# Attention in steps of four heads: the value product in plain float32, one key group in each half of TensorE's columns

## The chip, the cores and the metric

The kernel runs on one core of a Trainium2 chip. The metric is the device time of one execution in microseconds (us); lower is better. The engines are TensorE (PE for its matmuls, PEld for its weight loads), VectorE (DVE), ScalarE (ACT) and GpSimd (POOL); SyncE (SP) issues the DMAs.

## What is computed

Two layers of a backbone over 1024 latent and 256 context tokens of width 1024. The part that matters here is the attention of a layer: eight query heads of width 64 in two key groups, four heads to a group.

```python
def gqa_softmax(qg, k, v):
    s = jnp.einsum('bqgrd,bkgd->bgrqk', qg, k, preferred_element_type=jnp.float32) * (HEAD_DIM ** -0.5)
    p = jax.nn.softmax(s, axis=-1).astype(v.dtype)
    return jnp.einsum('bgrqk,bkgd->bqgrd', p, v)

def reference(...):
    for i in range(DEPTH):
        ...
        # latent queries read context and latent keys (1280), in both layers
        latent_attention(q, k, v, kc, vc)
        ...
        if update_ctx:      # layer 0 only: context queries read the 256 context keys
            context_attention(qc, kc, vc)
        ...
```

All arrays are float32. Pooling and Fourier mixers, an output projection, and a SwiGLU FFN fill the rest of a layer.

## The kernel before

**One list of operations, one planner.** The whole kernel is written as operations with an engine (or a choice of engines), a cost, and a rank; `Plan.run` (class at L53) takes them in order of time and rank and gives each engine its fixed sequence. `SHIFTS` holds an offset of rank for each name and layer, `ENGINES` the engines that a name may use, `ORDER` and `QUERY` the offsets inside one attention step. Buffers are slots that an operation takes and a later one gives back: pages of SBUF, two banks `t0`/`t1` for transposed tiles, one bank `sc` for context scores, one bank `pv` for the value product, two double banks `x0`/`x1` for latent scores.

**Most products are made in three parts.** TensorE multiplies float32 numbers that are split into a rounded high part (type F32R, "fp32r") and a rest (`mm3`, L473 to L475: low by high, high by low, high by high).

**Attention (from L1419).** A step is one *pair*: 128 queries (`t`), one key group `g`, two heads (`h0`, `h0`+1). A layer has 8 blocks of 128 latent queries, so 32 latent pairs; layer 0 has 8 context pairs more. For each pair:

- SC and SA/SB (`Pair.product`, L1502): scores, 4 matmuls of 256 columns for the context keys into `ps_sc`, and per head 4 of 512 columns into `ps_s`.
- MC, ML (L1511, L1431), N (L1435): maxima on DVE, and from them the bias of the exponential.
- EC, EL (L1441, L1447): exponentials on ACT, into `pc`/`pd` (context) and `p` (latent), with the row sums. R (L1517, L1518): reciprocal of the sum.
- T (L1461): five blocks of four 128x128 transposes, so that the keys lie in the partitions; each block of four is one bank `ps_t`.
- For blocks 0, 2 and 4 (`DIRECT`): ACT casts the bank to a high part `ph` (C), and DVE subtracts it from the bank for the low part (G). For blocks 1 and 3: ACT copies the bank to `pt` (C), ACT, DVE or POOL casts it (H), and POOL subtracts (G).
- V (L1484): the stationary operand is 128 columns wide, 64 columns of the values' high part and 64 of their low part for one group; the moving operand is 256 columns (two heads), once the high part, once the low part. So 20 matmuls for a latent pair, which run through all 128 columns of the array.
- F (L1523): the reciprocals are spread over 64 partitions by a float32 matmul with the identity, one per head, the two heads in the two column halves of the array.
- O (L1527), A (L1530), X (L1535): ACT copies the low half of `ps_pv`, DVE adds the high half and multiplies by the spread reciprocals.

The values are split into high and low parts once per layer (`value_chain`, L1001). The conditioning vector's products (`ada`, L560, matmul at L579) are float32 matmuls with a stationary operand of 32 columns, four of them side by side in the four quarters of the array; they are named because the prediction reads a price from them.

Of the kernel before, what the change touches and what calls it, by code (L numbers as in the profile page):

```python
# [17 lines left out]
P = 128  # L18
# [213 lines left out]
def ns_tt(n):  # L232
    return 68 + 1.043 * n
# [14 lines left out]

def ns_copy_psum(n):
    return 65 + 1.043 * n  # L250
# [16 lines left out]
def setting(table, name, default):  # L267
# [10 lines left out]

DIRECT = (0,2,4)
SPLIT = ()  # L280
OUT = "A"

DEFAULT = {"copy": "AD", "turn": "A", "sum": "DG", "shift": "AG", "square": "A"}
ENGINES = {"C": "A", "G": "G", "H": "ADG", "O": "A", "act hi": "A", "act lo": "DG", "act sum": "D", "eh": "AD", "el": "G",
# [5 lines left out]
           "pool lo": "D", "rope add": "DG", "rope cos": "DG", "rope sin": "DG", "square": "A", "sum": "D",  # L290
           "u hi": "G", "u lo": "DG", "v copy": "D", "v hi": "A", "w hi": "A", "w lo": "DG", "w sum": "DG",
           "x hi": "A", "x lo": "DG", "x shift": "AD", "x sum": "D"}

SHIFTS = ({"A": -523400, "C": -318500, "EC": -222000, "EL": -91800, "F": -234400, "G": -1299600, "H": -339200, "MC": -541600,
           "ML": -175000, "N": -423300, "O": -18300, "R": -17500, "SA": -9300, "SB": -491400, "SC": -1584400,
           "T": -718800, "V": 7200, "X": -457600, "aa": -1187200, "act hi": -456000, "act lo": -1226900,
           "act sum": 125700, "ada": -147400, "ada add": -15300, "ada row": -33000, "ada sum": 20100,
           "ada total": -857400, "ada turn": 12900, "as": 342600, "channels": -614600, "dft": -598800,
# [69 lines left out]
def tile_backbone(ctx: ExitStack, tc: tile.TileContext, i, out, x_spill, act_spill):  # L368
# [443 lines left out]
    def layer(l, x, hx, last_load):  # L812
# [188 lines left out]
        def value_chain(pair, o, first, e):  # L1001
# [11 lines left out]
            for j, ch in enumerate(pair):  # L1013
# [11 lines left out]
                def high(e, tag, b=b, v=v):  # L1025
                    v.t = page(tag, [n // P, 2, P], F32R, "v")
                    copy(e, v.t[:, :, :, 0:64], both(b.t))
# [1445 lines left out]
```

## Time and profile before

| | |
|---|---|
| time, median of 3 runs | 2696.35 us (2694.25 to 2696.66) |
| the profiled execution | 2692.95 us |
| its span, from the first instruction to the last | 2691.2 us |
| PE busy / DVE busy / ACT busy / POOL busy | 2589.1 / 2197.5 / 1302.1 / 723.0 us |
| mean granted TensorE clock | 0.987 of full speed |

How to read it: a row of a timeline gives start, duration, engine, source line, operation, output and input tiles and the number of merged instructions. The ends of matmuls are modelled and overlap, so the pace of TensorE is read from the distance between starts. A float32 matmul that isn't a transpose leaves two records; an fp32r matmul and a transpose leave one.

### The profile page before, as it was taken

Reading aid. Unit: us, or ns where it says so; the run is one execution under the profiler, and the core shown is the slowest. Engines: PE = TensorE matmul, PEld = TensorE weight load, DVE = VectorE, ACT = ScalarE, POOL = GpSimd, SP = SyncE. Lnnn points to the kernel's source line nnn. Section 1 sums busy time; section 2 is a strip of 40 time slices with the busy share of each in tenths; the row PEclk is TensorE's granted clock in tenths of the full one; section 3 lists DMA queues with packets and bytes.
Section 4 is the critical chain, followed back from the end, with each engine's and each line's share of the span. In section 5 each row is a group of like instructions: output and inputs, shape, how many; then the busy total and the mean of one; then the engine's idle time right before and its main releaser. Section 6 shows DMA issues by size and latency. Waiting matters only on the chain.

```text
span 2691.2 us, 39675 instructions
## 1 busy us (share of the span) xinstructions
PE 2589.1 (96%) x14670; PEld 2188.3 (81%) x14670; DVE 2197.5 (82%) x3681; ACT 1302.1 (48%) x2418; POOL 723.0 (27%) x578
## 2 busy tenths in 40 slices
PE   6999998998999999999999999999998999999999
PEld 5888887777788888888888888888876788888887
DVE  6765888889969988776788987888899977777886
ACT  4225987746522222233444534799846333333442
POOL 2113543464301100000223323444434401010240
PEclk8999999999999999999999999999998999999999
DMA  7244100245244445427534323000152332325733
GB/s 281 87 136 131 36 1 1 74 133 175 83 168 139 159 154 170 145 81 261 173 98 123 105 92 110 21 1 1 58 179 97 133 131 89 118 83 193 242 98 121
DMA packets 126210, 314.90 MB, mean 117 GB/s; under 512 B 14784, under 2 KB 23360, under 8 KB 126016
## 3 DMA queue, kind: packets, MB, share of 16 engines
q1 hardware_dynamic: 126016, 312.36, 34.9%
q8 instruction: 116, 1.90, 0.3%
q14 instruction: 78, 0.64, 0.1%
HBM read 244.94 MB, written 62.13 MB: 114 GB/s over the span
## 4 chain that ended last, share of the span: by engine, by line
PE 69%; DVE 18%; ACT 7%; issue 3%; DMA 3%; POOL 0%; SPq 0%; DVEq 0%; ACTq 0%; POOLq 0%
PE ps_s L473 7%; PE ps_s L474 7%; PE ps_s L475 7%; PE ps_d L474 5%; PE ps_d L473 5%; PE ps_d L475 5%; DVE half L463 3%; PE ps_pv L1484 3%; PE ps_in L473 3%; PE ps_in L474 3%; PE ps_in L475 3%; PE ps_t L1461 3%; PE ps_s L1502 2%; ACT p L1447 2%; DVE ws L463 2%
## 5 line engine op out<-in xcount | busy, mean ns | idle before, releaser
L460 ACT CAST half<-ws 128x512 fp32r<-128x512 f32 x410 | 246.5, 620 | 505.9 <-PE ps_s L475 220.5
L473 PE MATMUL ps_s<-half 128*128 128x512 f32 x1056 | 417.5, 395 | 15.4 <-DVE half L463 8.9
L474 PE MATMUL ps_s<-half 128*128 128x512 f32 x1056 | 416.3, 394 | 1.9 <-POOL half L463 1.2
L475 PE MATMUL ps_s<-half 128*128 128x512 f32 x1056 | 414.5, 393 | 0.0
L463 POOL TENSOR_TENSOR ws<-wst 128x512 f32<-128x512 f32 x95 | 147.2, 1551 | 922.2 <-DVE half L463 791.0
L473 PE MATMUL ps_d<-half 128*128 128x512 f32 (+1 forms) x792 | 290.0, 366 | 1.2 <-ACT half L460 1.2
L474 PE MATMUL ps_d<-half 128*128 128x512 f32 (+1 forms) x792 | 289.7, 366 | 1.0 <-DVE half L463 1.0
L475 PE MATMUL ps_d<-half 128*128 128x512 f32 (+1 forms) x792 | 289.5, 365 | 0.0
L463 DVE TENSOR_TENSOR half<-ws,half 128x512 fp32r<-128x512 f32 x324 | 232.9, 729 | 52.0 <-ACT half L460 49.6
L473 PEld LDWEIGHTS ps_s<-half 128*128 128x128 f32 x1056 | 200.7, 190 | 61.7 <-DVE half L463 9.9
L474 PEld LDWEIGHTS ps_s<-half 128*128 128x128 f32 x1056 | 200.5, 190 | 47.0 <-DVE half L463 3.4
L475 PEld LDWEIGHTS ps_s<-half 128*128 128x128 f32 x1056 | 200.6, 190 | 41.7
L463 POOL TENSOR_TENSOR ph<-pt,ph 128x512 fp32r<-128x512 f32 x128 | 164.2, 1283 | 234.2 <-DVE ph L460 105.7
L460 ACT CAST half<-wst 128x512 fp32r<-128x512 f32 x224 | 132.5, 618 | 191.5 <-PE ps_s L475 88.6
L1484 PE MATMUL ps_pv<-ph,v 128*128 128x256 f32 x1312 | 199.5, 291 | 4.3 <-DVE mix L1535 3.6
L463 POOL TENSOR_TENSOR half<-ws,half 128x512 fp32r<-128x512 f32 x86 | 122.2, 1429 | 263.5 <-ACT half L460 220.3
L1484 PEld LDWEIGHTS ps_pv<-ph,v 128*128 128x128 f32 x1312 | 174.2, 190 | 13.3 <-issue 3.2
L463 DVE TENSOR_TENSOR ws<-wst 128x512 f32<-128x512 f32 x235 | 166.4, 723 | 10.4 <-DMA wst<-in_w_gate_up 4.9
L473 PEld LDWEIGHTS ps_d<-half 128*128 128x128 f32 x792 | 149.4, 189 | 25.9 <-ACT half L460 1.6
L474 PEld LDWEIGHTS ps_d<-half 128*128 128x128 f32 x792 | 149.4, 189 | 25.4 <-DVE half L463 1.4
L475 PEld LDWEIGHTS ps_d<-half 128*128 128x128 f32 x792 | 149.4, 189 | 24.0
L463 DVE TENSOR_TENSOR half<-wst,half 128x512 fp32r<-128x512 f32 x211 | 142.0, 697 | 30.7 <-ACT half L460 30.6
(271 smaller groups left out, 6296.7 us busy)
## 6 DMA issues: line engine op xcount, KB each, us to landing
wst<-in_w_gate_up SPq DMA_DIRECT2D x99, 512.0 KB, 4.5
ast<-in_w_ada SPq DMA_DIRECT2D x96, 512.0 KB, 3.9
as<-act_spill SPq DMA_DIRECT2D x165, 256.0 KB, 2.7
hs<-in_w_out SPq DMA_DIRECT2D x96, 256.0 KB, 3.1
act_spill<-c SPq DMA_DIRECT2D x44, 512.0 KB, 5.1
wst<-in_w_down SPq DMA_DIRECT2D x44, 512.0 KB, 6.2
x_spill<-x SPq DMA_DIRECT2D x28, 512.0 KB, 3.1
x<-x_spill SPq DMA_DIRECT2D x26, 512.0 KB, 6.3
```

What stands on the lines that cost most here:

```text
L460: (nc.scalar.copy if e == "A" else nc.vector.tensor_copy)(out, x)
L463: (nc.vector if e == "D" else nc.gpsimd).tensor_tensor(out, x, y, op)
L473: nc.tensor.matmul(o, wl, xh, start=start, stop=False)
L474: nc.tensor.matmul(o, wh, xl, start=False, stop=False)
L475: nc.tensor.matmul(o, wh, xh, start=False, stop=stop)
L1447: nc.scalar.activation(self.p, self.s, AF.Exp, bias=pr.col(2, h), scale=rq[pr.at][:, h:h + 1], accum_out=pr.col(4, h))
L1461: nc.tensor.transpose(self.t[:, 2 * q + h, :], src, ident)
L1484: nc.tensor.matmul(pr.pv, v, m[:, 2 * q:2 * q + 2, :].rearrange("p h c -> p (h c)"), start=(self.k0 + q == 0 and j == 0), stop=(self.k0 + ...
L1502: nc.tensor.matmul(o, self.q[0][:, self.h0 + h, :], kv["k", k0](self.g, j), start=(j == 1), stop=(j == 0))
```

## The change

- A step is now a *quad*: two heads of both groups (`Quad`), made of two pairs. A layer has 16 latent quads; layer 0 has 4 context quads more.
- Values stay float32 and unsplit (`v out` in place of `v hi` and `v lo`), in two pages for a layer in place of three.
- Each transposed block is only copied, to a page `pt` that both groups share (C, on ACT or DVE). H, G and A are gone, with their buffers.
- V multiplies float32 by float32: for each tile of 128 keys one matmul for group 0 into partitions 0 to 63 of the bank and one for group 1 into partitions 64 to 127, each with 64 stationary and 256 moving columns. It is issued in two batches, blocks 0 and 1, then blocks 2, 3 and 4 with the spread F behind them (`BATCHES`).
- O copies 128 partitions at once, X multiplies once for the quad.
- Rings of buffers: `p` 5 (was 4), `ph` 7 (was 5), `qs` 4 in two pages (was 2), statistics `mx` 4 of double width; the page `b6` joins the rooms for `p` and `ph`.
- Nearly all numbers of `SHIFTS` and 32 entries of `ENGINES` are new, for the whole kernel; `ORDER` and `QUERY` are the same. One line of it:

```diff
-ENGINES = {"C": "A", "G": "G", "H": "ADG", "O": "A", "act hi": "A", "act lo": "DG", "act sum": "D", "eh": "AD", "el": "G",
+ENGINES = {"C": "AD", "G": "G", "H": "ADG", "O": "AD", "act hi": "A", "act lo": "D", "act sum": "D", "eh": "D", "el": "DG",
```

The core of the rest:

```diff
+def ns_fp32(n):
+    return 0.833 * n + 2
+NS_MODE = 300
-DIRECT = (0,2,4)
+BATCHES = ((0, 1), (2, 3, 4))
...
-                hi = op("turn", n, high, [t, pool_done[1]], take=[{256: "b5", 768: "b6", 0: "b7"}[ch]], name="v hi")
-                lo = op("D", ns_tt(n), lambda b=b, v=v: nc.vector.tensor_sub(
-                    v.t[:, :, :, 64:128], both(b.t), v.t[:, :, :, 0:64].bitcast(F32)), [hi], give=[t], name="v lo")
...
+                out_ = op("turn", n, lambda e, b=b, dst=dst: copy(e, dst(), b.t), [t, v.op], give=[t], name="v out")
...
-            def high(self, e, tag, x):
...
-            def low(self, e, x):
-                combine(e, self.l, x, self.h.bitcast(F32), ALU.subtract)
-            def values(self, *tag):
...
-                for q in range(2):
-                    v = kv["v", ch].t[:, self.k0 + q - ch // P, pr.g, :]
-                    for j, m in enumerate((self.h, self.l)):
-                        nc.tensor.matmul(pr.pv, v, m[:, 2 * q:2 * q + 2, :].rearrange("p h c -> p (h c)"),
...
+        class Quad:
...
+            def values(self, k0s, end, *tag):
...
+                for k0 in k0s:
+                    ch = max(c for c in SIZE if c <= k0 * P)
+                    for q in range(2):
+                        v = kv["v", ch]()[:, k0 + q - ch // P, :]
+                        for g in range(2):
+                            own = slice(64 * g, 64 * g + 64)
+                            nc.tensor.matmul(self.bank[own, 0:2 * P], v[:, own], self.pt[k0][:, g, 2 * P * q:2 * P * q + 2 * P],
+                                             start=(k0 + q == 0), stop=(k0 + q == self.nkt - 1))
...
+                if end:
+                    self.spread()
+            def spread(self):
+                for h in range(2):
+                    for g in range(2):
+                        r = self.small[:, 12 * g + 10 + h:12 * g + 11 + h]
+                        nc.tensor.matmul(self.bank[64 * g:64 * g + 64, (2 + h) * P:(3 + h) * P], r.to_broadcast([P, 64]), ident,
+                                         start=True, stop=True)
...
-        for ch, t, g in [(ch, t, g) for ch in ((256, 768) if last else CHS)
-                         for t in range(0, SIZE[ch], P) for g in range(2)]:
+        for ch, t in [(ch, t) for ch in ((256, 768) if last else CHS) for t in range(0, SIZE[ch], P)]:
...
+                        cp = mk("C", "turn", 512, bl.copy, tr, *turned.get(b, [])[:1], j=b, take=[ring("ph"), rooms] if g == 0 else (),
+                                give=[tr])
...
+                for bs in BATCHES if ch else ((0,),):
+                    end = bs[-1] == len(pr.blocks) - 1
+                    lv = mk("V", "PE", 4 * len(bs) * ns_fp32(2 * P) + NS_MODE + 4 * end * ns_fp32(P),
```

How the instructions move, in three places. In all of them `ps_t` is a transposed block, `ps_pv` the value product, `ps_s` and `ps_sc` latent and context scores.

TensorE, in the attention of layer 1. Before, most of one pair, from its second block of latent transposes on:

```order
L1461 MATMUL ps_t<-ident,p 128x128 x4
L1502 MATMUL ps_s<-kd,qs 128x512 x4
L1484 MATMUL ps_pv<-ph,v 128x256 x4
L1461 MATMUL ps_t<-ident,p 128x128 x8
L1484 MATMUL ps_pv<-ph,v 128x256 x8
L1523 MATMUL ps_pv<-ident,smalls 64x128 x2
```

Now, the second half of a quad:

```order
L1529 MATMUL ps_sc<-kd,qt 128x256 x4
L1529 MATMUL ps_s<-kd,qt 128x512 x2
L1466 MATMUL ps_t<-ident,pc 128x128 x4
L1466 MATMUL ps_t<-ident,p 128x128 x4
L1529 MATMUL ps_s<-kd,qt 128x512 x4
L1466 MATMUL ps_t<-ident,p 128x128 x8
L1490 MATMUL ps_pv<-pt,v 64x256 x12
L1500 MATMUL ps_pv<-ident,smalls 64x128 x4
```

The value product stood in three pieces between transposes and scores, 20 matmuls for a pair. Now 12 follow each other directly, with the four spreads behind them; the other 8 of the quad stand two blocks of transposes earlier. In the built order of layer 1 the matmuls of L1490 carry a wait of their own in 5 places; elsewhere the transposes ahead of them already waited for the copies that freed their banks.

ScalarE, in the attention of layer 1 (`p` and `pc`, `pd` are the exponentials). Before:

```order
L1447 ACTIVATE p,smalls<-ps_s,smalls,rq 128x1024
L460 CAST ph<-ps_t 128x512
L460 COPY pt<-ps_t 128x512
L460 CAST ph<-pt 128x512
L1441 ACTIVATE pd,smalls<-ps_sc,smalls,rq 128x256
```

Now:

```order
L466 COPY pt<-ps_t 128x512
L1446 ACTIVATE pc,smalls<-ps_sc,smalls,rq 128x256
L1452 ACTIVATE p,smalls<-ps_s,smalls,rq 128x1024
L466 COPY pt<-ps_t 128x512 x2
L1446 ACTIVATE pd,smalls<-ps_sc,smalls,rq 128x256
```

The two casts to `ph` are gone. Over the kernel ACT had 200 casts from `ps_t`, 128 copies of it and 48 casts of `pt`; now it has 212 copies, and DVE has 116.

GpSimd, towards the end of the attention of layer 0, where the queries of the context come. Before:

```order
L463 TENSOR_TENSOR qs<-mix,qs 64x256 x2
L463 TENSOR_TENSOR ph<-pt,ph 128x512 x3
L463 TENSOR_TENSOR qs<-mix,qs 64x512
L463 TENSOR_TENSOR ph<-pt,ph 128x512 x2
L458 TENSOR_SCALAR ph<-pt 128x512
```

Now, at the same place:

```order
L469 TENSOR_TENSOR half<-mix,half 128x512
L469 TENSOR_TENSOR qt<-mix,qt 64x256 x4
L469 TENSOR_TENSOR qs<-mix,qs 64x512 x2
L469 TENSOR_TENSOR qt<-mix,qt 64x512 x2
L469 TENSOR_TENSOR half<-mix,half 128x512 x3
```

The 128 subtractions for `ph` and 11 casts are gone from POOL; of attention it keeps the low parts of the queries (`qs`, `qt`).

## Rows read from the trace of the kernel before

**Rows 1.** The profile's page: busy time by engine (share of the span, instructions), TensorE's busy tenths and the granted clock in 40 slices of the span, and the shares of the chain of work that ended last.

```profile
PE 2589.1 (96%) x14670; PEld 2188.3 (81%) x14670; DVE 2197.5 (82%) x3681; ACT 1302.1 (48%) x2418; POOL 723.0 (27%) x578
...
PE   6999998998999999999999999999998999999999
...
PEclk8999999999999999999999999999998999999999
...
PE 69%; DVE 18%; ACT 7%; issue 3%; DMA 3%; POOL 0%; SPq 0%; DVEq 0%; ACTq 0%; POOLq 0%
```

**Rows 2.** Busy time in three stretches of attention, the first two in layer 0, the third in layer 1. Columns: stretch, length, busy us (and instructions) of PE, PEld, DVE, ACT, POOL, then granted clock, DMA share and GB/s.

```profile
300.00:400.00 100.00, 97.74 (x705) 83.89 (x704) 87.23 (x190) 90.07 (x188) 46.76 (x44) 1.00 0.01 1
400.00:500.00 100.00, 89.11 (x618) 76.14 (x618) 87.26 (x170) 78.77 (x165) 37.48 (x36) 0.98 0.02 6
1750.00:1850.00 100.00, 98.56 (x706) 84.18 (x705) 86.81 (x192) 92.26 (x193) 43.87 (x40) 1.00 0.00 1
```

**Rows 3.** The same three stretches for the value product alone (line L1484): PE, PEld, clock, DMA share, GB/s.

```profile
300.00:400.00 100.00, 38.99 (x260) 34.21 (x261) 1.00 0.01 1
400.00:500.00 100.00, 34.22 (x218) 29.13 (x218) 0.98 0.02 6
1750.00:1850.00 100.00, 38.01 (x254) 33.18 (x253) 1.00 0.00 1
```

**Rows 4.** Timeline of TensorE over one latent pair of layer 1: start, us, engine, line, operation, tiles, stationary and moving shape, count.

```profile
1806.40 0.44 PE L1523 MATMUL ps_pv<-ident,smalls 128*64 128x128 f32 x4
1806.77 0.66 PE L1461 MATMUL ps_t<-ident,p 128*128 128x128 f32 x4
1807.45 1.20 PE L1502 MATMUL ps_s<-kd,qs 128*128 128x512 f32 x4
1808.52 0.74 PE L1502 MATMUL ps_sc<-kd,qs 128*128 128x256 f32 x4
1809.11 0.27 PE L1461 MATMUL ps_t<-ident,pd 128*128 128x128 f32 x1
1809.21 0.27 PE L1461 MATMUL ps_t<-ident,pc 128*128 128x128 f32 x1
...
1809.46 1.20 PE L1484 MATMUL ps_pv<-ph,v 128*128 128x256 f32 x8
1810.50 0.60 PE L1461 MATMUL ps_t<-ident,p 128*128 128x128 f32 x4
1810.85 1.17 PE L1502 MATMUL ps_s<-kd,qs 128*128 128x512 f32 x4
1811.86 0.64 PE L1484 MATMUL ps_pv<-ph,v 128*128 128x256 f32 x4
1812.34 1.04 PE L1461 MATMUL ps_t<-ident,p 128*128 128x128 f32 x8
1813.13 1.20 PE L1484 MATMUL ps_pv<-ph,v 128*128 128x256 f32 x8
1814.26 0.44 PE L1523 MATMUL ps_pv<-ident,smalls 128*64 128x128 f32 x4
1814.63 0.66 PE L1461 MATMUL ps_t<-ident,p 128*128 128x128 f32 x4
```

**Rows 5.** Timeline of TensorE early in the run, around the float32 products of `ada` in four column quarters.

```profile
21.35 0.64 PE L579 MATMUL ps_ada<-ast,cond 128*32 128x128 f32 x16 [0.41 <-DVE rows L588]
...
22.24 1.52 PE L579 MATMUL ps_ada<-ast,cond 128*32 128x128 f32 x48
```

**Rows 6.** Timeline of TensorE where such products stand alone between fp32r matmuls of 512 columns.

```profile
200.51 0.39 PE L474 MATMUL ps_in<-parts,w 128*128 128x512 f32 x1
200.74 0.39 PE L475 MATMUL ps_in<-parts,w 128*128 128x512 f32 x1
201.06 0.64 PE L579 MATMUL ps_ada<-ast,cond 128*32 128x128 f32 x16
201.63 0.50 PE L473 MATMUL ps_in<-parts,w 128*128 128x512 f32 x1
```

**Rows 7.** Groups of instructions by line with the shapes kept apart: busy us, mean ns of one, idle time before them and what ended it.

```profile
L1431 DVE TENSOR_REDUCE smalls<-ps_s 128x1 f32<-128x1024 f32 x128 | 155.8, 1218 | 6.3 <-PE ps_s L1502 6.1
...
L460 ACT CAST ph<-ps_t 128x512 fp32r<-128x512 f32 x200 | 116.7, 585 | 20.1 <-PE ps_pv L1484 10.1 <-PE ps_t L1461 9.7
...
L463 POOL TENSOR_TENSOR ph<-pt,ph 128x512 fp32r<-128x512 f32 x128 | 164.2, 1283 | 234.2 <-DVE ph L460 105.7 <-ACT ph L460 102.1 <-issue 23.2
L1447 ACT ACTIVATE p<-ps_s,smalls,rq 128x1024 f32<-128x1024 f32 x128 | 155.9, 1218 | 0.1
...
L463 DVE TENSOR_TENSOR ph<-ps_t,ph 128x512 fp32r<-128x512 f32 x200 | 137.4, 687 | 24.2 <-ACT ph L460 18.1 <-POOL ph L463 0.5
...
L1441 ACT ACTIVATE pc<-ps_sc,smalls,rq 128x256 f32<-128x256 f32 x90 | 50.8, 565 | 16.8 <-DVE smalls L1435 11.4 <-PE ps_pv L1523 3.6 <-DVE smalls L1513 0.4
```

**Rows 8.** Timeline of all engines at one moment in layer 0's attention, GpSimd's and VectorE's rows.

```profile
406.13 1.28 POOL L463 TENSOR_TENSOR ph<-pt,ph 128x512 fp32r<-128x512 f32 x1 [4.87 <-ACT ph L460]
...
406.27 1.17 DVE L1435 SCALAR_TENSOR_TENSOR smalls<-smalls,nrq 128x1 f32<-128x1 f32 x1
```

**Rows 9.** Timeline of VectorE in layer 1's attention: the same operation as in the second row of the group above.

```profile
1812.35 0.21 DVE L1435 SCALAR_TENSOR_TENSOR smalls<-smalls,nrq 128x1 f32<-128x1 f32 x1
```

More of the change, by code (lines that the diff above doesn't have):

```diff
@@ L1575, in layer @@
             for h0 in (0, 2):
-                pr = Pair(ch, t, g, h0, q)
+                quad = Quad(ch, t, h0)
+                pairs = [Pair(quad, g, qs[g]) for g in range(2)]
                 def mk(kind, eng, ns, f, *after, j=0, take=(), give=(), alone=None):
@@ L1602, in layer @@
-                uses["k"][1].extend(read)
-                uses["k"][0].extend(read if ch else ())
-                join(ex, [(sc, 0)])
-                rc = mk("R", "D", 260, pr.recip, *ex, *el)
-                lv = None
-                first_v = None
-                for b, bl in enumerate(pr.blocks):
-                    tr = mk("T", "PE", 436, bl.transpose, *(el if b else ex), j=b, take=[TB])
-                    if b == 0:
-                        join([tr], ex)
-                    if b in DIRECT:
-                        hi = mk("C", "A", 478, lambda _, tag, bl=bl: bl.high("A", tag, bl.t), tr, j=b, take=[ring("ph"), rooms])
-                        lo = mk("G", "D", ns_tt(512), lambda bl=bl: bl.low("D", bl.t), hi, j=b, give=[tr], alone=True)
-                    else:
-                        cp = mk("C", "turn", 512, bl.copy, tr, fixed["pt"].op, j=b, take=[ring("pt")], give=[tr])
-                        hi = mk("H", "copy", 512, lambda e, _, tag, bl=bl: bl.high(e, tag, bl.pt), cp,
-                                j=b, take=[ring("ph"), rooms])
-                        lo = mk("G", "sum", 512, lambda e, bl=bl: bl.low(e, bl.pt), hi, j=b, give=[cp])
-                    lv = mk("V", "PE", 436, bl.values, lo, lv, *vd, j=b, take=["pv"] * (b == 0), give=[hi])
@@ new lines, in layer @@
+                lv = first_v = None
+                for bs in BATCHES if ch else ((0,),):
+                    end = bs[-1] == len(pr.blocks) - 1
+                    lv = mk("V", "PE", 4 * len(bs) * ns_fp32(2 * P) + NS_MODE + 4 * end * ns_fp32(P),
+                            lambda *tag, bs=bs, quad=quad, end=end: quad.values([2 * b for b in bs], end, *tag),
+                            *[c for b in bs for c in turned[b]], lv, *vd, *(rc if end else ()), j=bs[-1], take=["pv"] * (lv is None))
@@ L1621, in layer @@
                     first_v = first_v or lv
+                    join([lv], [turned[b][0] for b in bs])
                     uses["v"][1].append(lv)
                     uses["v"][0].extend([lv] if ch else ())
[L1624 to L1629 removed]
@@ L1630, in layer @@
-                join([fx_], [(sc, 1)])
+                o = mk("O", "turn", 256, quad.copy, lv, take=[ring("o")])
+                fx_ = mk("X", "D", ns_tt(256), quad.scale, o, give=[first_v, o])
+                join([fx_], [(small, 1)])
                 att.setdefault((ch, t), []).append(fx_)
-                n += 1 if ch else 0.4
-            join(read, [qh])
+            for g in range(2):
+                join(read[g], [qh[g]])
         plan.t = TB0 + 7000 * n
```

233 lines of the change are left out of this document (119 added, 114 removed), and 53 rows, old and new, of tables (ENGINES, SHIFTS).

## Prediction

> **What bounds the kernel now.** I read the page first. TensorE is busy for 96% of the span at nearly full clock, and of the chain that ended last 69% is TensorE's, 18% VectorE's [rows 1]. So only what shortens TensorE's sequence, or a wait in it, can pay, and I look for the stages where it is not packed. The change rewrites attention, so the stretches of attention come next. In layer 1, and in layer 0 from 300 to 400 us, three engines are nearly full at once: in 100 us TensorE is busy for 98, ScalarE for 90 to 92, VectorE for 87 [rows 2]. Such a stage turns in a ring: the scores wait for an exponential's buffer, the exponential queues behind casts on ScalarE, its bias behind subtractions on VectorE. From 400 to 500 us all is slower: TensorE 89, ScalarE 79 [rows 2], and 218 value matmuls pass instead of 260 [rows 3]. At 20 for a pair that is 10.9 pairs instead of 13.0, so 2.1 pairs of 100/13.0 = 7.7 us, or 16 us, are lost there.
>
> The timeline of one pair gives TensorE's prices [rows 4]. From 1806.77 to 1814.63 it takes 7.86 us. The value product takes 1.04 (1809.46 to 1810.50), 0.48 (1811.86 to 1812.34) and 1.13 (1813.13 to 1814.26), together 2.65; the spread takes 0.37 (to 1814.63). All the rest, scores and transposes, takes 7.86 - 3.02 = 4.84.
>
> **The change, part by part.** *A. Value product and spread on TensorE.* Two pairs become one quad: 2 x 3.02 = 6.04 us go. What comes is float32 products in two column halves, and the trace has the same kind in four quarters. There 16 records take 0.64 us and 48 take 1.52 [rows 5]: 32 records, 16 matmuls, four sets of four, in 0.88, so 0.22 for a set of 128 columns. That is what one fp32r matmul of 512 columns takes (200.51 to 200.74, 0.23) [rows 6]. The spread of today is two float32 matmuls in two halves, and 0.37 later TensorE is at the next transpose [rows 4]; one after the other they would need 2 x 0.22 before any change of shape is paid. So I take halves to overlap as quarters do: a set of two matmuls of 256 columns costs 0.44. The bounds are 0.44 and, with no overlap, 0.88; nothing lower, since 256 columns cannot pass sooner than twice 128. Going into such products and out of them costs too: alone between two others, two sets take from 200.74 to 201.63 = 0.89, of which 0.23 is the matmul before them and 0.44 the sets, so 0.22 for a visit [rows 6]. I take 0.22; the bounds are 0 and 0.5. A quad has 10 sets in two visits, and two sets of 0.22 for the spread in the second: 4.40 + 0.44 + 0.44 = 5.28. That saves 0.76, in 32 latent quads 24 us. A context quad goes from 2 x (4 x 0.1325 + 0.37) = 1.80 (a value matmul being 2.65/20) to 0.88 + 0.44 + 0.22 = 1.54; four of them save 1. **A: -25 us.**
>
> One rule of the skill speaks against this price. The rows show a set of four in the time of one, 0.22 [rows 5]. The Trainium skill, in "TensorE: Matmul & The Clock Gate", section "Measured speedup vs the span model", gives a speedup of 2.38 for three column tiles, which is 79% of three. As an estimate from that page a set would take 0.44/0.79 = 0.56, and the sum would come to about 2690 instead of 2651.
>
> *B. Waits in the ring.* By the built order ScalarE's 376 casts and copies of transposed blocks become 212; at 0.585 us [rows 7] the 164 gone are 96 us, 2.7 for each of the 36 quads. VectorE loses 200 subtractions of 0.687 and gains 116 copies, which I price like them (a read of the same bank): -58 us, and the additions and 69 casts besides. From about 90% of a quad both fall below 80%, so TensorE alone should set the pace. What can that give? The 4.84 us for the rest of a pair hold 20 transposes 0.11 apart (1809.11, 1809.21), 8 matmuls at 0.23 and 4 at half of that: 2.2 + 1.84 + 0.46 = 4.5. So 0.34 in a pair, 0.68 in a quad, 22 us in 32, is waits and starts. Part of it comes with each change of operand and stays. I take a third. **B: -8 us** (bounds 0 and -22).
>
> *C. The slow stretch of layer 0.* Its 16 us have a visible cause: a bias operation that takes VectorE 0.21 us [rows 9] takes 1.17 while GpSimd runs a subtraction for `ph` from 406.13 on [rows 8]. All 128 of these, 1.283 us each [rows 7], are gone. **C: -12 us**, not -16, since the stretch also holds waits of other kinds (bounds 0 and -16).
>
> *D. At nothing.* The values' high and low parts (a few operations of a chain with TensorE busy beside it), the copies O now for a whole quad, and equal numbers of scores, transposes and DMAs. The bank `pv` is held longer, but the next value batch stands a dozen rows of transposes and scores later. The new ranks move everything else too; FFN, with the matmuls end to end, cannot gain, other stages might by 10 either way. I take 0.
>
> Sum: -25 - 8 - 12 = -45 us on the profiled 2692.95 (span 2691.2 and 1.75 around it), 2648. The median of the runs stands 3.4 above that execution, so **2651 us**. A latent quad of layer 1 then takes 15.72 - 0.76 - 0.25 = 14.7 us.
>
> **The rivals.** *1. The exponentials' ring becomes the bound (slower).* A quad's heads share two double banks of scores. In the new order the third head's scores stand behind two groups of eight transposes, one of scores and the first batch: 0.79 + 1.01 + 0.79 [rows 4] + 1.98 = 4.6 us after the first head's. In that time must pass maximum 1.218, bias 0.21, two exponentials 0.565 and 1.218 [rows 7, 9], together 3.2, and some 0.5 of handovers. Slack: 0.9. Each copy that gets ahead on both queues costs 0.585 + 0.687 = 1.27. With two on each, 3.7 + 2.5 = 6.2 is 1.6 too late, 51 us in 32 quads: 2651 + 51 = 2702. It decides from 1.4 us of wait per quad on; below that the change still gains. For it: four heads bunched where a pair had two. Against it: copies may go to the freer engine, and the value batches carry a wait of their own in few places. Chance 0.09.
> *2. No overlap in the halves.* Each of 328 sets costs 0.44 more: 2651 + 144 = 2795. Today's spread speaks against it [rows 4]. Chance 0.04.
> *3. Overlap in part.* If the two halves share some of what feeds them, a set lies between 0.44 and 0.88; with a quarter of the way lost it costs 0.55, and 328 x 0.11 = 36 us go: 2687. The rows of four quarters speak against it [rows 5], though with 128 columns and not 256. Chance 0.05. (The skill's speedup named under A would give about this.)
> *4. Smaller gain.* The waits stay in another place, or the ranks cost something: A alone gives 2696.35 - 25 = 2671, with up to 15 lost besides. Chance 0.15.
> *5. Larger gain.* All of B and C and some from the ranks: -25 - 22 - 16 = -63, 2633, and lower with ranks that help. Chance 0.17.
> *6. Gain and loss cancel.* Half of rival 1: 2696. Chance 0.05.
>
> **How the numbers follow.** The forecast, 2636 to 2668, has the remaining 0.45. A measurement tells 0.2%, 5.4 us, from no change. Faster: 0.45 + 0.05 + 0.15 + 0.17 = 0.82. Same: 0.05. Slower: 0.09 + 0.04 = 0.13. The range goes from 2624, which holds most of case 5, to 2702, where rival 1 begins to lie outside; beyond it are rival 2, some of rival 1 and a little of case 5, under 2 in 10.
>
> **What would show it.** A: value records one after another at about 0.11 apart (four records for a set of 0.44), a batch of 16 records with its way in near 2.0 us. At 0.22 apart rival 2 holds. B: ScalarE and VectorE below 80% in attention, quads of 14.7 us in both layers; scores idle for an exponential by over 1 us per quad would be rival 1. C: no bias operation over 0.5 us, layer 0 at the pace of layer 1. If attention is shorter by 45 us and the time isn't, the ranks gave it back elsewhere. A gain that lies outside attention would make the prediction right for a wrong reason.

## The result, and the profile after

The changed kernel takes 2628.1 us (median of 4 runs, 2627.1 to 2629.2), beside 2695.3 for the kernel before (4 runs, 2690.6 to 2696.7): ratio 0.9754, 95% interval 0.9737 to 0.9771, 67 us less. The forecast was 2651 in a range of 2624 to 2702, faster with 0.82. Direction and range held, and 2628 lies below the narrower forecast of 2636 to 2668 that had 0.45. The gain is half as large again as the sum of 45. The runs below show that A and B had the wrong size, and that most of what they stand for has another cause than the one I named.

The changed kernel's code stands 6 lines lower in the helpers: V is L1490, F L1500, T L1466, scores L1529, the bias L1440, the exponentials L1446 and L1452. Of its page, busy time by engine, and the shares of the chain that ended last (to hold against [rows 1]):

```profile
PE 2545.8 (97%) x14670; PEld 2114.6 (81%) x14670; DVE 2085.6 (79%) x3283; ACT 1205.8 (46%) x2218; POOL 655.5 (25%) x498
...
PE 78%; DVE 13%; ACT 3%; DMA 3%; issue 2%; POOL 2%; SPq 0%; DVEq 0%; ACTq 0%; POOLq 0%
```

TensorE's share of the chain rises from 69% to 78%. The stretches of attention, all engines (start and end, length, then busy PE, PEld, DVE, ACT, POOL, granted clock, DMA share, GB/s), to hold against [rows 2]; then the value products' rows alone, against [rows 3]:

```profile
300.00:400.00 100.00, 100.00 (x782) 78.55 (x780) 72.53 (x144) 77.19 (x161) 11.21 (x15) 1.00 0.00 1
400.00:500.00 100.00, 97.70 (x773) 75.23 (x771) 71.62 (x141) 72.73 (x159) 15.79 (x15) 1.00 0.15 48
1700.00:1800.00 100.00, 99.76 (x774) 78.19 (x773) 68.65 (x137) 79.08 (x168) 13.79 (x17) 1.00 0.00 1
```

```profile
300.00:400.00 100.00, 33.31 (x280) 18.81 (x280) 1.00 0.00 1
400.00:500.00 100.00, 34.39 (x288) 19.34 (x288) 1.00 0.15 48
1700.00:1800.00 100.00, 33.30 (x280) 18.87 (x280) 1.00 0.00 1
```

ScalarE and VectorE are below 80%, and TensorE has hardly a gap. With 40 records to a quad, 280 are 7.0 quads in 100 us, where 260, 218 and 254 were 6.5, 5.5 and 6.4. The slow stretch of layer 0 is gone. TensorE over one quad of layer 1 (start, duration, engine, line, operation, tiles, shapes, count), to hold against the pair of [rows 4]:

```profile
1761.82 0.74 PE L1529 MATMUL ps_sc<-kd,qs 128*128 128x256 f32 x4
...
1766.00 1.03 PE L1466 MATMUL ps_t<-ident,p 128*128 128x128 f32 x8
1766.96 1.95 PE L1490 MATMUL ps_pv<-pt,v 128*64 128x256 f32 x16
1768.84 0.73 PE L1529 MATMUL ps_s<-kd,qs 128*128 128x512 f32 x2
...
1772.15 1.03 PE L1466 MATMUL ps_t<-ident,p 128*128 128x128 f32 x8
1773.12 2.81 PE L1490 MATMUL ps_pv<-pt,v 128*64 128x256 f32 x24
1775.76 0.61 PE L1500 MATMUL ps_pv<-ident,smalls 128*64 128x128 f32 x8
1776.30 0.39 PE L1529 MATMUL ps_sc<-kd,qs 128*128 128x256 f32 x1
```

The quad takes 14.48 us (1761.82 to 1776.30). V and F take 1.88 + 3.18 = 5.06 where 5.28 was forecast.

Where the 64.5 us of span went, from the first and last rows of each kind of product in TensorE's timelines (us, before and after): in-projection of layer 0 257.7 and 255.2; its attention to the last latent score 257.0 and 220.0; the rest of it with the output projection 144.4 and 142.0; FFN 872.6 and 877.2; in-projection of layer 1 156.4 and 160.2; its attention 258.4 and 237.5; output projection 82.5 and 81.1; FFN 662.2 and 653.6. So 61.7 of the 64.5 lie in attention with its output projections, and the new ranks have moved the rest by 2.7 in all (FFN of layer 0 is 4.6 slower, that of layer 1 8.6 faster).

A part of the 61.7 can be the clock. In these stages the granted clock fell to 0.50, its lower level of 1.2 GHz, five times before, for 3.4 us each, and not once after. Each fall came behind waits of TensorE. The first of them, with the ten us ahead of it (stretch, length, busy PE, granted clock, DMA share, GB/s):

```profile
444.50:454.50 10.00, 8.05 (x58) 1.00 0.00 0
454.50:457.90 3.40, 3.40 (x15) 0.50 0.00 0
```

At half the pace for 3.4 us a fall costs at most 1.7 us, so at most 8.5 of the 61.7 are the clock's.

To see what a quad is made of, I take the time from each of TensorE's records to the next, put it down to the kind of the first, and keep the profile's idle time apart, over 11 to 13 quads of layer 1 (two pairs count as a quad):

| kernel, layer 1, us per quad | all | scores | transposes | V | F | idle |
|---|---|---|---|---|---|---|
| before | 15.93 | 5.35 | 4.35 | 5.26 | 0.74 | 0.23 |
| after | 14.64 | 5.13 | 4.40 | 4.52 | 0.54 | 0.06 |
| after, V in fp32r | 14.75 | 5.02 | 4.05 | 5.04 | 0.59 | 0.06 |
| before, no subtractions | 15.72 | 5.34 | 4.31 | 5.27 | 0.74 | 0.06 |
| before, no subtractions, light casts | 15.70 | 5.34 | 4.31 | 5.27 | 0.74 | 0.04 |
| after, two more visits | 15.48 | 5.21 | 5.20 | 4.52 | 0.54 | 0.02 |
| after, ScalarE's copies twice | 16.28 | 5.28 | 4.95 | 4.52 | 0.54 | 0.99 |

In layer 0 (from 290 us on) the quad goes from 16.78 to 14.48. The lower rows are the experiments.

### The profile page after: what moved, and what is told of

Read it like the earlier page. It is cut to its first block, busy times and chain, and to the rows that moved or that the text cites. A ratio compares the mean times of both kernels' runs of the same rounds, so it can differ in the third digit from the quotient of the medians.

```text
span 2626.7 us, 38814 instructions
## 1 busy us (share of the span) xinstructions
PE 2545.8 (97%) x14670; PEld 2114.6 (81%) x14670; DVE 2085.6 (79%) x3283; ACT 1205.8 (46%) x2218; POOL 655.5 (25%) x498
## 4 chain that ended last, share of the span: by engine, by line
PE 78%; DVE 13%; ACT 3%; DMA 3%; issue 2%; POOL 2%; SPq 0%; DVEq 0%; ACTq 0%; POOLq 0%
PE ps_s L479 7%; PE ps_s L480 7%; PE ps_s L481 7%; PE ps_d L479 6%; PE ps_d L480 6%; PE ps_d L481 6%; PE ps_pv L1490 6%; PE ps_t L1466 5%; PE ps_s L1529 5%; DVE half L469 3%; PE ps_in L479 3%; PE ps_in L480 2%; PE ps_in L481 2%; DVE ws L469 2%; PE ps_sc L1529 1%
## 5 line engine op out<-in xcount | busy, mean ns | idle before, releaser
L469 POOL TENSOR_TENSOR half<-ws,half 128x512 fp32r<-128x512 f32 x114 | 167.2, 1473 | 555.0 <-ACT half L466 459.0
L469 POOL TENSOR_TENSOR ws<-wst 128x512 f32<-128x512 f32 x127 | 198.9, 1572 | 411.5 <-DVE half L469 333.4
L469 DVE TENSOR_TENSOR half<-ws,half 128x512 fp32r<-128x512 f32 x296 | 214.7, 745 | 50.8 <-ACT half L466 49.8
L1436 DVE TENSOR_REDUCE smalls<-ps_s 128x1 f32<-128x1024 f32 x128 | 156.2, 1222 | 36.0 <-PE ps_s L1529 34.7
L479 PE MATMUL ps_in<-parts,w 128*128 128x512 f32 (+1 forms) x416 | 158.9, 382 | 1.6 <-DVE parts L466 1.6
L480 PE MATMUL ps_in<-parts,w 128*128 128x512 f32 (+1 forms) x416 | 154.7, 372 | 2.9 <-POOL parts L469 2.8
L1490 PE MATMUL ps_pv<-pt,v 128*64 128x256 f32 x1312 | 156.4, 384 | 1.0 <-DVE rows L594 1.0
```

Source lines behind the costliest of these rows:

```text
L469: (nc.vector if e == "D" else nc.gpsimd).tensor_tensor(out, x, y, op)
L479: nc.tensor.matmul(o, wl, xh, start=start, stop=False)
L480: nc.tensor.matmul(o, wh, xl, start=False, stop=False)
L1436: nc.vector.tensor_reduce(self.pair.col(1, self.h), self.s, AX.X, ALU.max)
L1490: nc.tensor.matmul(self.bank[own, 0:2 * P], v[:, own], self.pt[k0][:, g, 2 * P * q:2 * P * q + 2 * P], start=(k0 + q == 0), stop=(k0 + q = ...
```

## Experiments

**1. The groups one after the other.** Inside a batch, group 0 first, then group 1.

```diff
-                for k0 in k0s:
-                    ...
-                        for g in range(2):
+                for g in range(2):
+                    own = slice(64 * g, 64 * g + 64)
+                    for k0 in k0s:
```

> The changed kernel, with the same instructions on every engine, but inside a batch all value matmuls of group 0 come first (left half of the array), then all of group 1 (right half). Theory: the change pays because two matmuls in different halves run at the same time; a record takes 0.105 us, so a set of two matmuls 0.42. Without a neighbour in the other half a set costs 0.84 to 0.88: 328 sets x 0.42 to 0.46 = +138 to +151 us, about 2628 + 145 = 2773, and a batch of 16 records takes 3.5 us instead of 1.88. Rival: a float32 matmul with 64 stationary columns is that cheap wherever its neighbour stands (0.21 for 256 columns): no change, 2628.

Measured: 2712.1 us, ratio to before 1.0063 (1.0043 to 1.0084): 84 us more than the change. The halves do run at the same time, and apart they lose, but only part of what I expected. Where one half works alone, its records of 256 columns follow each other by 0.216 us; in alternation a pair of records, one in each half, takes the same 0.216. Timeline of TensorE around the end of a quad:

```profile
1820.10 3.94 PE L1490 MATMUL ps_pv<-pt,v 128*64 128x256 f32 x21
1823.66 0.43 PE L1500 MATMUL ps_pv<-ident,smalls 128*64 128x128 f32 x2
1823.87 0.59 PE L1490 MATMUL ps_pv<-pt,v 128*64 128x256 f32 x2
1824.09 0.43 PE L1500 MATMUL ps_pv<-ident,smalls 128*64 128x128 f32 x2
1824.30 0.38 PE L1490 MATMUL ps_pv<-pt,v 128*64 128x256 f32 x1
1824.52 0.60 PE L1500 MATMUL ps_pv<-ident,smalls 128*64 128x128 f32 x4
```

F, issued last, begins between value products of the other half. A half that has its operands starts before the other is done, so some overlap remains without alternation: a batch of 16 takes 2.79 us (1830.20 to 1832.99), between 1.88 in alternation and twice that.

**2. The product alone: fp32r in the new order.**

```diff
-                        for g in range(2):
-                            own = slice(64 * g, 64 * g + 64)
-                            nc.tensor.matmul(self.bank[own, 0:2 * P], v[:, own], self.pt[k0][:, g, ...], ...)
+                        for g in range(4):
+                            nc.tensor.matmul(self.bank[:, 0:2 * P], v, self.pt[k0][:, g // 2, ...], ...)
```

> The changed kernel in its own order, but V issues per tile of keys four fp32r matmuls of 128 stationary and 256 moving columns, which is what the kernel before issued for two pairs (the split itself is left out: the operands are only rounded, so the output is not the reference's). It prices step A alone. Theory: a set goes from 0.42 to 4 x 0.131 = 0.525, and the first of two visits per quad costs nothing more: 328 x 0.105 - 32 x 0.2 = +28, 2656. Rival: TensorE's pace in V was not where the time came from; with waits elsewhere setting the step the time stays within 10 of 2628.

Measured: 2631.2 us, ratio 0.9766 (0.9750 to 0.9782), 3 more than the change, whose interval it overlaps. My theory fell. Its timeline:

```profile
1771.94 1.03 PE L1466 MATMUL ps_t<-ident,p 128*128 128x128 f32 x8
1772.73 1.17 PE L1529 MATMUL ps_s<-kd,qs 128*128 128x512 f32 x4
1773.74 1.03 PE L1466 MATMUL ps_t<-ident,p 128*128 128x128 f32 x8
1774.53 2.16 PE L1489 MATMUL ps_pv<-pt,v 128*128 128x256 f32 x16
1776.53 0.63 PE L1529 MATMUL ps_s<-kd,qs 128*128 128x512 f32 x2
1777.00 0.63 PE L1529 MATMUL ps_sc<-kd,qs 128*128 128x256 f32 x4
```

The batch of 16 takes 2.00 instead of 1.88. But the eight transposes ahead of it take 0.79 here (1773.74 to 1774.53) and 0.96 in the change (1766.00 to 1766.96), and the two scores behind it 0.47 here, 0.57 there. The float32 halves are 0.57 cheaper per quad in V and F, and give back 0.35 in the transposes and 0.11 in the scores beside them. Net 0.11, or 3.5 us in 32 quads: that is all that the new arithmetic itself is worth on TensorE in the new order.

**3 and 4. One batch, five batches.**

```diff
-BATCHES = ((0, 1), (2, 3, 4))
+BATCHES = ((0, 1, 2, 3, 4),)
```

> The changed kernel with all five blocks of a quad in one value batch, so one visit to the float32 products instead of two; the order around it is made anew by the planner. Theory (a visit costs 0.2 us): 32 x 0.2 = 6.4 us less, 2622. Rival: the batch stands later, holds its pages and the bank longer, and waits for the last copy: slower than 2628, by 16 us if it is half a us per quad.

Measured: 2699.1 us, ratio 1.0018 (1.0009 to 1.0027). The rival was right: a quad of layer 1 takes 16.12, of which 1.58 idle, for exponentials and for copies.

```diff
-BATCHES = ((0, 1), (2, 3, 4))
+BATCHES = ((0,), (1,), (2,), (3,), (4,))
```

> The changed kernel with one value batch per block, so five visits per quad instead of two. Theory: 3 x 32 x 0.2 = 19 us more, 2647. Rival: smaller batches come sooner, free their pages sooner and leave fewer waits: no more than 2628. If a visit cost nothing the time would be 2628 as well; the spacing around a batch tells these two apart.

Measured: 2667.9 us, ratio 0.9903 (0.9887 to 0.9920), 40 more than the change and twice what I expected. But the quad of layer 1 is longer by only 0.46; the end of layer 0's attention with its output projection (154.8 instead of 142.0), FFN of layer 1 (445.4 instead of 439.3) and layer 0's attention itself (231.4 instead of 220.0) hold most of the rest. The planner had moved too much; the price of a visit does not follow from it.

**5 and 6. The kernel before without subtractions.** The low half becomes two columns, and the value product takes the high half twice; every engine's order stays.

```diff
-                combine(e, self.l, x, self.h.bitcast(F32), ALU.subtract)
+                s, self.l = ((slice(None), 3, slice(126, 128)), self.h) if e == "G" else (slice(None), self.l); combine(e, self.l[s], x[s], self.h[s].bitcast(F32), ALU.subtract)
```

> The kernel before, every engine's order unchanged, but GpSimd's 128 subtractions of blocks 1 and 3 shrink from 512 columns to 2, and the value product takes the rounded half twice (so the low half of these blocks is left out of the result). It prices step C. Theory: the slow stretch of layer 0 comes from operations of VectorE that are held up beside these subtractions; 12 to 16 us go there, no bias operation over 0.5 us is left between 399 and 504 us, layer 1 gains little: about 2695 - 14 = 2681. Rival: the stretch is slow for the weights' loads and other work beside it; the time stays at 2695 within 4.

Measured: 2684.9 us, ratio 0.9956 (0.9942 to 0.9971), 10 less. In the profiles 8.3 lie in layer 0's attention and 2.1 in layer 1's. Of 128 bias operations 12 took over 0.5 us before, 9 of them in layer 0; 3 do here, 2 of them in layer 0. Windows of all engines, as above:

```profile
400.00:500.00 100.00, 91.80 (x656) 78.75 (x656) 83.25 (x180) 83.94 (x177) 16.17 (x40) 1.00 0.02 6
1750.00:1850.00 100.00, 98.78 (x708) 84.42 (x707) 86.93 (x193) 92.12 (x192) 17.54 (x41) 1.00 0.00 1
```

From 400 to 500 us TensorE is at 91.80 where it had 89.11 [rows 2]; in layer 1 hardly anything moves. Step C's cause holds, for 8.3 of the (16.78 - 15.93) x 16 = 13.6 us that layer 0's quads had lost; up to 1.7 of the 8.3 can be the fall of the clock shown above, which this run does not have.

The second run shrinks VectorE's subtractions too (the condition is always true).

> The kernel before, order unchanged, with VectorE's 200 subtractions of transposed blocks shrunk to 2 columns as well (their low halves are left out of the result). It adds step B's part on VectorE. Theory: VectorE falls from 87% to about 70% in attention and the waits in the ring shrink, by 8 to 15 us beyond the run without GpSimd's subtractions: about 2670. Rival: TensorE's own sequence sets the step there and VectorE's load was covered; the same as without GpSimd's subtractions, 2681 or wherever that run comes out.

Measured: 2678.2 us, ratio 0.9936 (0.9917 to 0.9954). VectorE is at 72.66 from 1750 to 1850 us instead of 86.81 [rows 2], and the quad of layer 1 falls by 0.21 only, 0.17 of it idle time. VectorE's load was not what held the ring in layer 1.

**7. ScalarE's copies twice in the change.**

```diff
-                copy(e, pr.quad.pt[self.k0][:, pr.g, :].rearrange("p (a b) -> p a b", b=P), self.t)
+                for _ in range(1 + (e == "A" and self.k0 != 8)): copy(e, pr.quad.pt[self.k0][:, pr.g, :].rearrange("p (a b) -> p a b", b=P), self.t)
```

> The changed kernel, order unchanged, with ScalarE's load brought back to about that of before: every copy of a transposed block that ScalarE makes, except of the last block, is made twice. In the layer 1 quads of before, 0.33 us of scores, 0.30 of transposes and 0.17 of idle time are over what the same products take in the changed order, 0.80 x 32 = 26 us. Theory: these are waits for ScalarE's queue, and come back with the load: 2628 + 16 to 26, about 2649, ScalarE near 90% in attention. Rival: they came from the order of the steps (two heads at a time) and not from the load: within 6 of 2628.

Measured: 2681.6 us, ratio 0.9952 (0.9940 to 0.9964): 53 more, above both guesses. The waits from 1700 to 1900 us (engine, tile and line, what it waited for: us, times, longest):

```profile
PE ps_t L1466 <- ACT pt L466: 11.9, 26, 0.9
```

The change has one such wait of 0.2 us from 1700 to 1860. They are not waits for an exponential, but of transposes for a bank whose copy is not done. Two banks for transposes bear one copy of 0.585 us, not two. This run therefore says nothing of the old ring; it says that the new order needs the short copy, which the change made by dropping the split.

**8 and 9. The kernel before with light casts.** Beside the subtractions, ScalarE's casts of blocks 0, 2 and 4 shrink to two columns.

```diff
-                copy(e, self.h, x)
+                s = (slice(None), 3, slice(126, 128)) if self.k0 in (0, 4, 8) else slice(None); copy(e, self.h[s], x[s])
...
-                    for j, m in enumerate((self.h, self.l)):
+                    for j, m in enumerate((self.h, self.l) if self.k0 in (2, 6) else (pr.q[0], pr.q[0])):
```

> The kernel before, order unchanged, without the subtractions' work on GpSimd and VectorE and without ScalarE's casts of blocks 0, 2 and 4 (all shrunk to 2 columns; the value product of these blocks takes the queries' page in their place, so the output is not the reference's and these products wait for nothing). Beside the run without subtractions it takes off ScalarE's part of step B alone. Theory (the ring's waits are ScalarE's load): 0.5 to 0.8 us per quad go, 16 to 26 us: 2678 - 20 = about 2658. Rival (the waits are in the order of the steps): no less than 2672.

Measured: 2694.8 us, ratio 1.0003 (0.9993 to 1.0013). This says little, since value products now waited for GpSimd's work on the queries' page (20 times from 1700 to 1900 us, 5.6 us in the profile). The second version takes the values' page in its place:

> As the last light version of the kernel before (no work in the subtractions, none in ScalarE's casts of blocks 0, 2 and 4; order unchanged), but these blocks' value products take the values' own page in place of the queries', so that no wait for the queries is put in (the output is not the reference's). Theory of ScalarE's load: its share falls from 90% to about 72%, and 0.5 to 0.8 us per latent quad go beside the run without subtractions: 2678 - 16 to 26, about 2657. Theory of the order: in the order before, the next pair's scores wait for an exponential that ScalarE has behind its copy of block 3, and that copy waits for TensorE's transposes; this loop (transposes, copy 0.59, exponential 1.21, scores) holds however light the casts are: 2672 to 2682, with the exponential still next behind that copy.

Measured: 2669.2 us, ratio 0.9911 (0.9895 to 0.9928), 9 less than without the subtractions, between the two theories. In the profiles 5.6 of it lie in layer 0's attention, where the quads from 400 to 500 us fall from 17.14 to 16.23. In layer 1 ScalarE falls from 92.66 to 79.32 and the quad stays, 15.72 and 15.70. Timelines of this run, TensorE and ScalarE:

```profile
1806.52 1.04 PE L1461 MATMUL ps_t<-ident,p 128*128 128x128 f32 x8
...
1809.49 1.20 PE L1502 MATMUL ps_s<-kd,qs 128*128 128x512 f32 x4
```

```profile
1807.65 0.59 ACT L460 COPY pt<-ps_t 128x512 f32<-128x512 f32 x1 [0.33 <-PE ps_t L1461]
1808.14 1.21 ACT L1447 ACTIVATE p<-ps_s,smalls,rq 128x1024 f32<-128x1024 f32 x1
```

The order shows. ScalarE idles for the transposes of block 3, copies them, and only then runs the exponential whose end (1809.35) lets the next scores start at 1809.49. No lighter cast can shorten that. The weight loads of the scores over 22 pairs, from 1722.4 to 1895.2 us (count, busy, mean ns, idle before), still waited 5.6 us for an exponential, 0.51 per quad:

```profile
L1502 PEld LDWEIGHTS ps_s<-kd,qs 128*128 128x128 f32 x176 | 29.7, 189 | 9.6 <-ACT p L1447 5.6
```

**10. The kernel before with a cheaper spread.**

```diff
-                for h in range(2):
-                    nc.tensor.matmul(self.rb[h], self.col(5, h).to_broadcast([P, 64]), ident, start=True, stop=True)
...
+                for h in range(2 if self.k0 == pr.nkt - 2 else 0): nc.tensor.matmul(pr.bank[:, (2 + h) * P:(3 + h) * P], v, self.h[:, h, :], start=True, stop=True)
```

> The kernel before, its other rows in the same order; each pair's spread F, two float32 matmuls in the two halves of the array, is replaced by two fp32r matmuls of 128 stationary and 128 moving columns right behind the last value matmul (the reciprocals are left out of the result). Theory: going into products in column halves and back to whole ones costs time by itself, and in the kernel before it is paid once per pair around F: 0.209 instead of 0.120 us into F, 0.203 out of it, and the first scores after it start 0.29 instead of 0.03 after the transpose ahead of them. With some 0.5 us per pair, 32 latent pairs and something for 8 context pairs give 16 to 18 us: 2694 - 17 = 2677. Rival: the late scores wait for an exponential, and the spread's price is its own 0.37 alone, of which the new matmuls take 0.12 to 0.25: 4 to 10 us, 2684 to 2690.

Measured: 2696.4 us, ratio 0.9997 (0.9983 to 1.0011): nothing. This is the run that decides. Timeline of TensorE, then the weight loads of the scores from 1726 to 1906 us (count, busy, mean ns, idle before):

```profile
1801.66 0.34 PE L1487 MATMUL ps_pv<-ph,v 128*128 128x128 f32 x2
1801.83 0.62 PE L1461 MATMUL ps_t<-ident,p 128*128 128x128 f32 x4
1802.96 1.21 PE L1503 MATMUL ps_s<-kd,qs 128*128 128x512 f32 x4 [0.51 <-ACT p L1447]
...
1809.85 0.62 PE L1461 MATMUL ps_t<-ident,p 128*128 128x128 f32 x4
1810.82 1.20 PE L1503 MATMUL ps_s<-kd,qs 128*128 128x512 f32 x4 [0.34 <-ACT p L1447]
```

```profile
L1503 PEld LDWEIGHTS ps_s<-kd,qs 128*128 128x128 f32 x181 | 30.6, 188 | 18.3 <-ACT p L1447 14.3
```

The spread costs TensorE 0.17 instead of 0.37, and the time turns into waits for the exponential, 14.3 us in 22.6 pairs, twice as much for a pair as before (below). From scores to scores it is 1810.82 - 1802.96 = 7.86, as in the pair of [rows 4]; on average over 1715 to 1912 us a pair takes 7.95, and took 7.96 before. In layer 1 the kernel before was bound by the loop, not by the sum of TensorE's work, although TensorE was 98.56 busy there. The loop itself runs through TensorE: in [rows 4] the stretch from the scores at 1807.45 to the transposes at 1812.34, 4.89 us without a gap, belongs to it. The spread lies outside that stretch, beside the copy and the exponential.

**11. Two more visits in the change.**

```diff
+                for j in range(2 if self.k0 == 8 else 0):
+                    nc.tensor.matmul(self.t[64 * j:64 * j + 64, 0, :], ident[:, 64 * j:64 * j + 64], ident, start=True, stop=True)
```

> The changed kernel, its other rows in the same order; ahead of the last block's transposes of each latent pair stand two more float32 matmuls of 64 stationary and 128 moving columns, one in each half, whose result the transposes overwrite. So two more visits per quad. By their own pace in a batch the two take 0.11 us: 32 quads x 2 x 0.11 = 7 us, 2635, if a visit costs nothing more. Theory A (a visit between transposes costs some 0.15 more, as the run with five batches has it): 2628 + 32 x 2 x 0.26 = 2645. Theory B (a visit costs 0.4 more wherever it stands): 2628 + 32 x 2 x 0.51 = 2661.

Measured: 2657.1 us, ratio 0.9861 (0.9847 to 0.9876): 29 for 64 visits, 0.45 each; by the quads it is 0.84 for two, 0.42 each. One visit in TensorE's timeline:

```profile
1798.74 0.74 PE L1531 MATMUL ps_sc<-kd,qs 128*128 128x256 f32 x4
1799.41 0.44 PE L1464 MATMUL ps_t<-ident 128*64 128x128 f32 x4
1799.78 0.66 PE L1468 MATMUL ps_t<-ident,p 128*128 128x128 f32 x4
```

The expectation put the products too low. They leave four records, two pairs, and in a batch pairs of 128 columns follow each other by 0.109 (the spreads of the change), so the two take 0.22 and not 0.11. A visit then costs 0.20 more by the quads and 0.23 by the time, between theory A's 0.15 and theory B's 0.40 and nearer A. Here TensorE's time counts: the quad grows by what the visits take, so the changed kernel is bound by TensorE in layer 1.

**12. The old ranks outside attention.** In the change, the offsets and choices of engine of before for all names outside attention.

> The changed kernel, with the offsets of rank and choices of engine of before for every name outside attention; attention's own are those of the change. Theory: by the stages of the two traces 56 of the 64 us lie in attention and its output projection, and 8 outside; so about 8 us are given back, 2636. Rival: the new ranks outside carry far more, through what they let attention find ready: 2650 or more. If they carry nothing: 2628.

Measured: 2660.2 us, ratio 0.9873 (0.9848 to 0.9899), 32 more. It doesn't price the ranks. Its FFN of layer 0 ahead of the down projection (598.8) is slower than both parents' (592.8 and 593.3), and its attention of layer 0 gets 9 worse though no rank of attention differs: the offsets fit one another. The opposite mixture was not run.

## Why the prediction was right, and where its steps were not

**A, forecast -25: mis-sized, and the reason fell.** V and F went from 6.00 to 5.06, which is more than forecast, and a set costs 2.64/6 = 0.44 as said. What was mis-sized is the two visits of a quad, put at 0.44 inside V and F. By the pace in a batch (0.216 and 0.109 for a pair of records) the products take 4.32 + 0.44, so 0.30 of the visits stands inside V and F; 0.35 and 0.11 more stand in the transposes before V and the scores behind it, held against the fp32r run. That makes 0.76. Counted with the rows beside V, A is 0.94 - 0.46 = 0.48 per quad, 15 us. And 0.37 of that is not float32 at all: the fp32r run has 5.63 for V and F in the same order, by larger batches and one spread for two pairs. The rule of the Trainium skill that I weighed against A ("TensorE: Matmul & The Clock Gate", section "Measured speedup vs the span model") would, by the estimate there, have had a set at 0.56; the trace has 0.44, so the two halves overlapped fully, and the trace decides. What did bear on A is the price of going in and out. The Trainium skill says in "TensorEngine Tiling (Array Packing)", section "Key Properties", that a change of the tiling mode drains TensorE. The runs agree so far as going in and out costs time, 0.20 us for a visit in the run with two more of them; that a drain is what costs it, no row tells.

**B, forecast -8, bound -22: mis-sized, and the cause named was wrong for most of it.** Between before and the fp32r run, scores, transposes and idle time fall by 0.33 + 0.30 + 0.17 = 0.80 per quad, 26 us, which is beyond the bound. I put the waits down to the load of ScalarE and VectorE. The runs with light subtractions and light casts show that in the old order this load was worth 0.23 per quad. The other 0.57 went only with the new order. The old one has a loop: transposes of block 3, copy, exponential, next scores. The rows of before have it (timeline of all engines, with the weight loads, which [rows 4] leave out):

```profile
1804.48 1.04 PE L1461 MATMUL ps_t<-ident,p 128*128 128x128 f32 x8
...
1805.12 0.59 ACT L460 CAST ph<-ps_t 128x512 fp32r<-128x512 f32 x1
...
1805.61 0.59 ACT L460 COPY pt<-ps_t 128x512 f32<-128x512 f32 x1
...
1806.10 1.21 ACT L1447 ACTIVATE p<-ps_s,smalls,rq 128x1024 f32<-128x1024 f32 x1
...
1807.45 0.76 PEld L1502 LDWEIGHTS ps_s<-kd,qs 128*128 128x128 f32 x4 [0.26 <-ACT p L1447]
```

The exponential ends at 1807.31, the scores start at 1807.45. The groups of weight loads say how often, before (22 pairs from 1726.7 to 1901.9 us) and after (13 quads from 1675.4 to 1865.6 us):

```profile
L1502 PEld LDWEIGHTS ps_s<-kd,qs 128*128 128x128 f32 x176 | 29.7, 189 | 11.0 <-ACT p L1447 7.1
```

```profile
L1529 PEld LDWEIGHTS ps_s<-kd,qt 128*128 128x128 f32 x112 | 18.5, 189 | 5.2 <-issue 2.7 <-ACT p L1452 0.7
L1529 PEld LDWEIGHTS ps_s<-kd,qs 128*128 128x128 f32 x96 | 16.0, 189 | 4.4 <-issue 1.9 <-ACT p L1452 0.7
```

Scores waited 7.1 us in 22 pairs for an exponential, 0.65 per quad, and still 0.51 with light casts; now 1.4 in 13 quads, 0.11. So these waits can be up to 0.40 of the 0.57; the other 0.17 is not traced. Nor is it shown that the order alone would do: with every copy made twice the new order loses 53 us (experiment 7), so it needs the short copies too. TensorE's own rows of before show 1.9 of the 7.1: a matmul's modelled end covers the start of the next wait. I had read 0.34 per pair of "waits and starts" from them and kept a third. The Trainium skill, in "Perfetto Trace Analysis", section "Identifying the Most-Contended Engine", says that a matmul's busy share is no good measure of how near a kernel is to the roofline, and points to that of the weight loads, among others, instead. This trace agrees: 98.56 busy and 84.18 for the weight loads [rows 2], in a stretch that a loop held. Reading the idle time ahead of the weight loads is this case's own step.

**A and B are not independent.** The spread run shows that in the old order 0.20 off the spread of a pair is worth nothing, since it stands beside the copy and the exponential; the last value batch of the pair stands there too. The other two, 1.52 of the value product's 2.65, stand in the 4.89 us of TensorE that the loop runs through, and there a saving should have shortened the loop. No run tried that, so how much of A the old order would have paid stays open. For layer 1 the sum was near (a quad of 14.7 forecast, 14.64 measured), but by errors that met: A too large by 0.28, B too small by 0.55, and the quad before 15.93 on average where the one pair that I had read gives 15.72.

**C, forecast -12: right in cause, a little small.** Layer 0's quads lost 0.85 to layer 1's before, 13.6 us in 16; after, they are 0.16 faster, which makes 16. Without GpSimd's subtractions 8.3 go in the profiles, without VectorE's nothing more, and with ScalarE's casts light as well another 5.6. The clock blurs these steps: over layer 0's attention it fell once before, not at all without GpSimd's subtractions, twice without VectorE's, and not at all with light casts. At 1.7 us at most for a fall, up to 1.7 of the 8.3 and up to 3.4 of the 5.6 can be the clock, and VectorE's part can be up to 3.4. All the same, load did count in this stretch: with all of it light the same ten pairs, from about 400 us on, take 16.84 per quad where they took 18.64. Three bias operations still take over 0.5 us after, one of them in layer 0.

**Sum.** 15 + 26 + 16 = 57 of the 61.7 in attention; the other 4.7 are left to context quads, stage ends and the clock. D, at nothing, measured 2.7, the balance of FFNs and in-projections that moved by up to 8.6 each.

**Rivals.** 1 did not come (0.11 per quad where it needed 1.4); the one-batch run shows what it looks like when it does. 2 and 3 are out: two halves take the time of one. 4 and 6 are out. 5, the larger gain, comes nearest with 2633, C at its bound as there; but A was 15 where it has 25, and B 26 where it has 22.

**Open** is which part of the change broke the loop: four heads in flight, the fifth page for exponentials, the batches, or the short copies with them. The runs with one and with five batches were too much rearranged to tell, and pairs as before under new ranks were not run.

## What to carry to other kernels

When every engine of a stage is near 90% busy, look for a loop before adding up costs: follow one late start back through the other engines' order, and read idle time ahead of the weight loads, where modelled matmul ends don't hide it. Make one engine's work cheaper in the old order. If the time doesn't move, that work is not on the loop: only a shorter step of the loop or a new order will pay, and a cheaper operation is worth what it makes possible in that order. Price a visit to column-tiled products with the rows on both sides of it, and make few of them.

## What the runs showed of the hardware that I had not expected

- Two float32 matmuls in the two column halves cost the time of one: 24 records of 256 columns in 2.64 us, 0.22 for a pair of records, and 0.216 for one record where a half works alone. Sixteen records, eight of one half ahead of eight of the other, still overlap in part: 2.79 us, where alternation takes 1.88.
- Sixteen fp32r matmuls of 256 columns in one batch take 2.00, 0.50 for the four that a set replaces, so unsplit float32 in halves, at 0.44, is only an eighth cheaper than the split product.
- A visit to products in column halves costs 0.20 us beyond the products between scores and transposes; around the value products two visits cost 0.76.
- A bias operation of one column, 0.21 us alone, took 1.17 beside GpSimd's subtraction of 512 columns [rows 8, 9]; without the 128 subtractions for `ph` the kernel before is 10 us faster.
